# Moving the later modulation products beside the long convolutions and the scan

## The chip, the cores and the metric

The kernel runs on one core of a Trainium2 chip. The metric is the device time of one execution in microseconds; a time of a kernel is the median of its runs. The profile is of one further execution.

## The reference

Two layers of a trunk work on 1152 tokens (1024 latent, 128 prompt) of width 1024, in fp32. Each layer first computes six modulation vectors per condition (there are two conditions, `c` for latent tokens and `c_ctx` for prompt tokens), and then uses them around the token mixing and around the MLP:

```python
mod = einsum('bd,de->be', silu(cond), w_ada) + b_ada          # 1024 -> 6*1024
sh1, sc1, gt1, sh2, sc2, gt2 = split(mod, 6)
h = rms_norm(x, g_pre_mix) * (1 + sc1) + sh1
o = mixer(h)        # latent attention, windowed attention, gated delta scan, long convolutions
x = x + gt1 * rms_norm(o, g_post_mix)
h = rms_norm(x, g_pre_mlp) * (1 + sc2) + sh2
m = square(relu(h @ mlp_w1)) @ mlp_w2
x = x + gt2 * rms_norm(m, g_post_mlp)
```

`w_ada` is 1024 x 6144 per layer, 24 MB in fp32, and serves two rows of input: there is much to load and little to compute.

## The kernel before

The program is traced from Python and laid out by a planner. Every instruction goes to a fixed engine; the planner orders each engine's instructions by the order in which the Python code emitted them and by when it believes their inputs and buffers to be ready, and adds the waits. SP issues all DMAs, in its own order. On the chip each engine then works through its fixed list.

**Modulation products.** `ada(l, g)` (line 386) computes group `g` of layer `l`: 2048 columns, that is two of the six vectors. Group 0 holds `sh1, sc1`, group 1 `gt1, sh2`, group 2 `sc2, gt2`. It takes eight steps, one per 128 rows of weights. A step loads four tiles `wada` of 128x512 (256 KB each) and multiplies each by the condition, which stands as a 128x32 weight tile; the four results go to four strips of 32 partitions of one PSUM tile from tag P, which stays taken until the group ends. A ninth step copies the result to a row (`adarow`), transposes it in four pieces (`adat`) and adds the bias. The tiles `wada` come from tag T, which has four buffers, or from the tag given.

**Order of emission.** In each layer `run_timed` (line 2149) emits three generators side by side. Each has a clock of its own; the one with the lowest clock goes next, and each `yield` moves its clock on by the number yielded, or by a default.
- `rest()` is the main line: projections (15 units for each tile), then `hyena` (line 1682, two long convolutions through DFT matmuls, 10 units a step, eleven steps), then `attention` (line 1003, 2 units a step). Attention's main part begins only when `"other"` is done.
- `other()` is the gated delta rule: filters, `gdn_prep` and `gdn_scan` (line 1292, 16 steps in sequence), 6 units a step, emitted with a priority raised by 300.
- `adas()` (line 2055) waits 580 units (`SIDE`) and then emits groups 1 and 2 of this layer at 12 units a step, which falls beside attention.

The first group of layer 0 is computed at the start of the kernel. The first group of layer 1 is emitted beside the MLP of layer 0 (lines 2128 and 2129), with `wada` in the six buffers of tag H. The MLP itself runs in 16 blocks of two 128-row tiles of hidden units.

**Names in the rows.** `ada`, `wada`, `wo` (weights of the output projection, staged in tag T by `load_rows`, line 236), `op` (the output projection's PSUM), `S` and `ST` (scores of latent attention, for the maximum and for the weights), `O` (its output), `u` and `St` (vector and state of the scan), `sc` (the scan's loaded operands), `hid` and `mo` (MLP). Tags P, T and H have 4, 4 and 6 buffers.

Of the kernel before, what the change touches and what calls it, by code (L numbers as in the profile page):

```python
# [19 lines left out]
DEPTH = 2  # L20
# [7 lines left out]
GD = 6  # L28
PL = 4
AT = 2  # L30
SIDE = 580
NCH = ((0, 384), (384, 384), (768, 384))


# [130 lines left out]
class Trunk:  # L165
# [1830 lines left out]
    def layer(self, l):  # L1996
# [31 lines left out]
        def filters(tag, psum, h=None):  # L2028
            if h is None:
                h = self.W(name="sines", tag=tag)  # L2030
                nc.sync.dma_start(out=h[64 * l:64 * l + 64], in_=self.fscr[64 * l:64 * l + 64])
            for _ in self.hy_filters(l, h, self.dft_mats("fwd", tag), tag, psum):
                yield 8
# [15 lines left out]
        g, be = self.gdn_shared(l, gab, self.gdn_tag)  # L2049
# [2 lines left out]
                self.late_consts()  # L2052
        self.done = set()

        def adas():
            yield SIDE
            for a in (1, 2):
                yield from self.ada(l, a)

        def until(x):  # L2060
            while x not in self.done:
                yield 1

        def rest():
            yield from self.proj_gdn(l, hi, lo, (2, 4, 0), gcw, head)
            self.done.add("gdn0")
            yield from self.proj_rest(l, hi, lo, gab, gcw)
            self.small, self.other = R[0][-1], R[1][-1]
            first = self.mla_prep(l, 0)
            yield from self.hyena(l, self.sink(l), lambda: next(first))  # L2070
            yield from self.attention(l, first)

        def other():
            yield from filters(self.gdn_tag, "Q") if l else early
            yield from until("gdn0")
            self.pair = {}
            yield from self.gdn_prep(l, 0, g, be, self.gdn_tag)
            yield from until("gdn")
            yield from self.gdn_prep(l, 1, g, be, self.gdn_tag)
            yield from until("z")  # L2080
            yield from self.gdn_scan(l, self.gdn_tag)
            self.done.add("other")

        def ahead(g):
            while True:
                with self.tc.high_priority(300):
                    t = next(g, "end")
                if t == "end":
                    return
                yield t  # L2090
        run_timed((rest(), 1.5), (ahead(other()), GD), (adas(), 12))
        self.small, self.other = R[0][-1], R[1][-1]
        op = self.out_proj(l, R[1])
        if "oT" in self.dbg and l == self.dbg.get("l", 1):
# [18 lines left out]
        for ts in range(7):  # L2113
            g = op([ts])
# [4 lines left out]
        g = op([7, 8])  # L2119
        out = next(g)  # L2120
        self.run((g, 1), (group(0, xs[0:3]), 1), (group(1, xs[3:6]), 1))
        g = self.mlp(l, hi, lo)
# [2 lines left out]
        next(g)  # L2125
        self.run((group(2, xs[6:]), 1))
        acc = next(g)
        nxt = self.ada(l + 1, 0, "H") if l + 1 < DEPTH else iter(())
        self.run((g, 1), (nxt, 0.7))
        gate2 = {}  # L2130

        def tail(t):
# [16 lines left out]
def run_timed(*gens):  # L2149

    gens = [[0.0, i, g, n] for i, (g, n) in enumerate(gens)]
    while gens:
        e = min(gens)
        try:
            t = next(e[2])
            e[0] += e[3] if t is None else t
        except StopIteration:
            gens.remove(e)
# [33 lines left out]
```

## Time and profile before

| | us |
|---|---|
| median of 3 runs (3913.01 to 3923.71) | 3920.94 |
| the profiled execution | 3901.65 |
| its span, first to last instruction | 3899.9 |
| TensorE busy in the span | 3570.1 |
| VectorE busy | 2260.8 |
| ScalarE busy | 1359.3 |
| GpSimd busy | 848.4 |

All rows below are of the profiled execution, and their times count from the first instruction. A mean granted clock of 1.00 is 2.4 GHz; a lower mean says that the engine stood at the 1.2 GHz level for a part of the stretch. TensorE's matmuls overlap in their pipeline and their ends are modelled, so the time from one start to the next is the better measure of what a matmul takes.

### The profile page before, as it was taken

To read this page: it belongs to the slowest core of one execution; us is meant where nothing else is said; L and a number is where in the kernel's file an instruction comes from. 1 tells how busy PE (TensorE), PEld (TensorE's weight loads), DVE (VectorE), ACT (ScalarE), POOL (GpSimd) and SP (SyncE) were. 2 spreads that over 40 slices of the span, in tenths; PEclk is the share of its full clock that TensorE was granted. 3 is DMA by queue.
4 is the path that set the end of the run, shared out by engine and by line. 5 is a ranking of instruction groups with operands and counts; after the bars stand their busy time and mean duration, and the time that the engine had idled before them with its cause. 6 is when DMAs were issued, how large, how long until landed. Compare 5 with 4: busy or idle time off the path is not lost. (4 is left out here: it accounts for less than half of the span.)

```text
span 3899.9 us, 57406 instructions
## 1 busy us (share of the span) xinstructions
PE 3570.1 (92%) x21674; PEld 2999.4 (77%) x21674; DVE 2260.8 (58%) x4583; ACT 1359.3 (35%) x2932; POOL 848.4 (22%) x806
## 2 busy tenths in 40 slices
PE   7989887799999999999979897768998999999997
PEld 4889765566689888888868886556565899999996
DVE  5766478776454444444566674878664544444446
ACT  5434433445442222112354343324454422222122
POOL 1152421454230000000131633225542200000003
PEclk9999886799999999999989998768999999999999
DMA  5355462452621111111234365633525211111113
GB/s 202 113 130 155 147 231 88 123 138 73 207 77 64 55 62 44 59 53 55 80 112 140 105 164 150 212 109 93 154 72 194 71 55 44 44 44 41 41 41 116
DMA packets 366399, 405.30 MB, mean 104 GB/s; under 512 B 116007, under 2 KB 237349, under 8 KB 366122
## 3 DMA queue, kind: packets, MB, share of 16 engines
q1 hardware_dynamic: 366122, 401.64, 33.6%
q8 instruction: 170, 2.79, 0.3%
q14 instruction: 107, 0.88, 0.1%
HBM read 298.34 MB, written 103.19 MB: 103 GB/s over the span
## 5 line engine op out<-in xcount | busy, mean ns | idle before, releaser
L214 PE MATMUL hid<-hT,w1h 128*128 128x384 f32 x3072 | 787.2, 335 | 0.1
L1821 DVE TENSOR_TENSOR acc<-acc,mo 128x512 f32<-128x512 f32 x540 | 370.0, 687 | 435.3 <-PE mo L214 435.2
L214 PE MATMUL pj<-hT,wah 128*128 128x384 f32 x2112 | 575.1, 349 | 10.2 <-ACT hc L517 7.8
L214 PEld LDWEIGHTS hid<-hT,w1h 128*128 128x128 f32 x3072 | 557.5, 188 | 21.6 <-issue 6.7
L214 PE MATMUL hid<-hT,w1l 128*128 128x384 f32 x1536 | 514.4, 335 | 0.0
L214 PE MATMUL mo<-w2h,uh 128*128 128x512 f32 x1152 | 450.8, 391 | 1.4 <-DVE acc L1821 1.4
L214 PE MATMUL mo<-w2l,uh 128*128 128x512 f32 x1152 | 451.1, 392 | 0.0
L214 PE MATMUL mo<-w2h,ul 128*128 128x512 f32 x1152 | 450.8, 392 | 0.0
L214 PEld LDWEIGHTS pj<-hT,wah 128*128 128x128 f32 x2112 | 392.6, 194 | 24.0 <-ACT hc L517 8.8
L270 POOL TENSOR_TENSOR postr<-postr,mhalf 128x1 f32<-128x1 f32 x36 | 22.4, 625 | 1642.7 <-DVE postr L269 903.3
L660 POOL TENSOR_TENSOR e<-e,e 128x512 f32<-128x512 f32 (+1 forms) x216 | 296.9, 1376 | 331.3 <-ACT e L649 215.3
L214 PE MATMUL pj<-hT,wal 128*128 128x384 f32 x1056 | 365.3, 346 | 0.7 <-DVE wal L233 0.7
L214 PEld LDWEIGHTS hid<-hT,w1l 128*128 128x128 f32 x1536 | 288.2, 188 | 2.5
L233 DVE TENSOR_TENSOR el<-e,eh 128x512 fp32r<-128x512 f32 (+1 forms) x252 | 247.3, 1002 | 57.8 <-ACT eh L651 54.1
L243 ACT CAST w2h<-w 128x512 fp32r<-128x512 f32 x128 | 71.2, 618 | 524.9 <-PE mo L214 520.8
L214 PEld LDWEIGHTS mo<-w2h,ul 128*128 128x128 f32 x1152 | 216.2, 188 | 47.3
L1803 ACT ACTIVATE relu<-hid 128x384 f32<-128x384 f32 x192 | 93.9, 489 | 443.4 <-PE hid L214 443.4
L214 PEld LDWEIGHTS mo<-w2h,uh 128*128 128x128 f32 x1152 | 216.4, 188 | 41.4 <-DVE acc L1821 1.8
L214 PEld LDWEIGHTS mo<-w2l,uh 128*128 128x128 f32 x1152 | 216.2, 188 | 38.8
L214 PEld LDWEIGHTS pj<-hT,wal 128*128 128x128 f32 x1056 | 205.0, 194 | 4.6 <-issue 2.0
L1804 DVE SCALAR_TENSOR_TENSOR relu<-hid,relu 128x384 f32<-128x384 f32 x192 | 106.2, 554 | 164.6 <-ACT relu L1803 164.4
L233 DVE TENSOR_TENSOR wal<-wa,wah 128x512 fp32r<-128x512 f32 x88 | 67.8, 772 | 166.3 <-ACT wah L254 132.3
(488 smaller groups left out, 6357.0 us busy)
## 6 DMA issues: line engine op xcount, KB each, us to landing
w<-in_w SPq DMA_DIRECT2D x256, 256.0 KB
wada<-in_w_ada SPq DMA_DIRECT2D x192, 256.0 KB
wa<-in_wa SPq DMA_DIRECT2D x88, 256.0 KB
x<-in_x SPq DMA_DIRECT2D x18, 512.0 KB
Q<-rscr SPq DMA_DIRECT2D x32, 288.0 KB
o<-oscr SPq DMA_DIRECT2D x18, 512.0 KB
xres<-x SPq DMA_DIRECT2D x36, 256.0 KB
x<-xres SPq DMA_DIRECT2D x36, 256.0 KB
```

The source lines that it names most:

```text
L214: self.last = self.nc.tensor.matmul(out, l, r, start=start, stop=stop, skip_group_check=True)
L233: self.nc.vector.tensor_tensor(out=lo, in0=x, in1=hi.bitcast(F32), op=ALU.subtract)
L243: self.nc.scalar.copy(out=hi[:, q], in_=st)
L270: self.nc.gpsimd.tensor_tensor(out=out, in0=out, in1=self.bcs(self.mhalf[:out.shape[0]], out.shape), op=ALU.pow)
L660: self.nc.gpsimd.tensor_tensor(out=acc, in0=acc, in1=e, op=ALU.add)
L1803: nc.scalar.activation(out=r[:, :n], in_=ps[:, :n], func=AF.Relu)
L1804: nc.vector.scalar_tensor_tensor(out=r[:, :n], in0=ps[:, :n], scalar=0.0, in1=r[:, :n], op0=ALU.max, op1=ALU.mult)
L1821: nc.vector.tensor_tensor(out=acc[t][:, ns], in0=acc[t][:, ns], in1=ps, op=ALU.add)
```

## The change

Groups 1 and 2 of a layer no longer wait 580 units; they begin when the projections of the layer have been emitted (`"proj"`), and each step moves their clock on by 5 instead of 12. In layer 0, group 0 of layer 1 follows them there, in tag T, and is gone from beside the MLP.

```diff
-SIDE = 580
...
-        def adas():
-            yield SIDE
-            for a in (1, 2):
-                yield from self.ada(l, a)
-
         def until(x):
             while x not in self.done:
                 yield 1

+        def adas():
+            yield from until("proj")
+            for a in ((l, 1), (l, 2)) + (((l + 1, 0),) if l + 1 < DEPTH else ()):
+                for _ in self.ada(*a):
+                    yield 5
+
         def rest():
             yield from self.proj_gdn(l, hi, lo, (2, 4, 0), gcw, head)
             self.done.add("gdn0")
             yield from self.proj_rest(l, hi, lo, gab, gcw)
+            self.done.add("proj")
...
-        run_timed((rest(), 1.5), (ahead(other()), GD), (adas(), 12))
+        run_timed((rest(), 1.5), (ahead(other()), GD), (adas(), 1))
...
-        nxt = self.ada(l + 1, 0, "H") if l + 1 < DEPTH else iter(())
-        self.run((g, 1), (nxt, 0.7))
+        self.run((g, 1))
```

## Rows read from the trace of the kernel before

**Rows 1.** The page: 40 slices of 97.5 us, TensorE busy and clock, tenths.

```profile
PE   7989887799999999999979897768998999999997
...
PEclk9999886799999999999989998768999999999999
```

**Rows 2.** Stretches: length; busy PE, PEld, DVE, ACT, POOL; clock; DMA share; GB/s.

```profile
530.00:704.00 174.00, 112.33 (x1102) 87.56 (x1102) 135.27 (x417) 52.47 (x179) 36.43 (x38) 0.69 0.48 150
760.00:816.00 56.00, 54.10 (x266) 42.45 (x265) 49.68 (x70) 33.75 (x63) 35.31 (x24) 0.94 0.36 83
816.00:847.00 31.00, 31.00 (x110) 13.62 (x109) 21.54 (x35) 10.94 (x21) 15.23 (x11) 1.00 0.51 155
869.00:896.00 27.00, 27.00 (x82) 10.71 (x81) 13.72 (x25) 11.52 (x20) 12.74 (x10) 1.00 0.36 107
954.00:1012.00 58.00, 58.00 (x252) 28.71 (x251) 29.31 (x42) 27.80 (x54) 24.50 (x21) 1.00 0.52 158
...
2460.00:2640.00 180.00, 116.00 (x1132) 89.72 (x1132) 135.33 (x420) 53.24 (x183) 37.33 (x38) 0.69 0.50 153
2753.00:2788.00 35.00, 35.00 (x121) 14.68 (x119) 24.39 (x41) 13.48 (x25) 15.61 (x11) 1.00 0.53 158
2806.00:2829.00 23.00, 23.00 (x68) 9.19 (x67) 12.67 (x20) 10.62 (x19) 11.91 (x9) 1.00 0.33 100
2890.00:2950.00 60.00, 58.81 (x255) 29.21 (x253) 29.90 (x45) 29.45 (x58) 24.86 (x21) 1.00 0.53 163
```

**Rows 3.** Tile ada: passes, ns min/median/max, first and last start; four stretches.

```profile
L214 PE MATMUL ada<-wada,cst x64: 592/617/1062, 12.7 to 38.5; 128*32 128x512 f32 x64
...
L214 PE MATMUL ada<-wada,cst x128: 592/605/617, 816.2 to 1011.6; 128*32 128x512 f32 x128
...
L214 PE MATMUL ada<-wada,cst x128: 592/605/617, 2753.5 to 2948.0; 128*32 128x512 f32 x128
...
L214 PE MATMUL ada<-wada,cst x64: 592/605/617, 1282.9 to 1772.7; 128*32 128x512 f32 x64
```

**Rows 4.** Timeline of TensorE in attention: start, us, instruction; two pieces, their followers.

```profile
816.25 1.07 PE L214 MATMUL ada<-wada,cst 128*32 128x512 f32 x8
817.25 0.73 PE L214 MATMUL ST<-Q,K 97*128 97x512 f32 x2
...
822.24 1.04 PE L214 MATMUL ada<-wada,cst 128*32 128x512 f32 x2
823.22 0.45 PE L214 MATMUL S<-K,Q 96*128 96x384 f32 x1
```

**Rows 5.** Tiles hid and mo: first and last matmul of each layer's MLP.

```profile
L214 PE MATMUL hid<-hT,w1h x1536: 333/334/445, 1126.7 to 1912.5; 128*128 128x384 f32 x192
L214 PE MATMUL mo<-w2h,ul x576: 387/393/473, 1139.8 to 1938.2; 128*128 128x512 f32 x192
...
L214 PE MATMUL hid<-hT,w1h x1536: 331/334/443, 3079.1 to 3853.5; 128*128 128x384 f32 x192
L214 PE MATMUL mo<-w2h,ul x576: 387/389/475, 3092.1 to 3879.8; 128*128 128x512 f32 x192
```

**Rows 6.** End of attention: SP's timeline, stretches as in 2, and TensorE's longest wait.

```profile
2940.08 1.74 SPq L393 DMA_DIRECT2D wada<-in_w_ada  x2
2942.89 1.97 SPq L242 DMA_DIRECT2D wo<-in_w_out  x2
...
1012.00:1050.00 38.00, 35.03 (x154) 27.33 (x154) 17.43 (x32) 16.61 (x31) 3.65 (x4) 0.96 0.85 288
2948.00:3000.00 52.00, 40.62 (x159) 28.45 (x158) 23.06 (x42) 21.87 (x43) 8.20 (x8) 0.93 0.71 246
...
PE op L214 <- ACT woh L243: 5.7, 7, 2.0
```

**Rows 7.** Waits from 530 to 704 us: total us, times, longest; SP, then TensorE.

```profile
SPq L1374 <- DVE sc L1371: 22.6, 5, 10.8
...
PE u L214 <- DVE u L1352: 10.1, 6, 2.9
```

## Prediction

> **What bounds the kernel now.** I read the page's slices first: TensorE stands at 9 all through the later attention and the MLP, and falls to 6 and 7 in slices 7 and 8 and again in 26 and 27, where the long convolutions and the scan of each layer run; the granted clock falls there too [rows 1]. Then the table by stretches. From 530 to 704 us and from 2460 to 2640 us, where the convolutions stand beside the scan, TensorE is busy 112.3 of 174 us and 116.0 of 180 us at a mean granted clock of 0.69, so part of the time at the 1.2 GHz level, while VectorE is busy 135 us in each (75 to 78%) [rows 2]. In the stretches of attention that hold the modulation products TensorE is busy all or nearly all of the time at full clock and VectorE only half to 70% [rows 2]. In the MLP TensorE is the bound outright [rows 1]. So the change takes TensorE work out of stretches that TensorE bounds and puts it where TensorE stands idle for 61.7 and 64.0 us.
>
> **What a product costs today.** One group of products is 32 matmuls of 512 columns, each shown as two passes. A layer has 128 passes in its attention, and 64 more lie in the first layer's MLP [rows 3]. Four matmuls write four different strips of 32 PSUM partitions; issued together they take 1.00 us up to the start of the next instruction (816.25 to 817.25), and a single one takes 0.98 us (822.24 to 823.22) [rows 4]. What counts is therefore the number of pieces. The timeline shows the 128 passes of a layer's attention in 52 pieces, 27 of the first group and 25 of the second: in each group one piece of eight passes, two or four of four, the rest of two. The reason is the buffers: weights come through the four slots of tag T, a slot is loaded again only when its matmul is done, and each matmul runs as soon as its load lands. In the MLP all eight pieces hold eight passes.
>
> **Part by part.** 1. *Out of attention.* 104 pieces of 0.98 us are 102 us of TensorE time, the most that can come back. Not all will, since VectorE comes next: where no product runs, at 760 to 816 us, it is busy 49.68 of 56 us, 89%, and I take that as its practical limit [rows 2]. For each stretch I take the larger of two floors: its TensorE time without the pieces, and its VectorE time over 0.887. 816 to 847 us has 15 pieces: 31 − 14.7 = 16.3 against 21.54/0.887 = 24.3, so 6.7 us saved. 869 to 896 has 12: 15.2 against 15.5, so 11.5 saved. 954 to 1012 has 25: 33.5 against 33.0, so 24.5 saved. In layer 1 the same working gives 7.5 (17 pieces), 8.7 (10) and 24.5 (25). Sum 83 us.
> 2. *Out of the MLP.* The MLP of layer 0 runs from 1126.7 to 1938.2 us, that of layer 1, which has no products in it, from 3079.1 to 3879.8: 811.5 − 800.7 = 10.8 us [rows 5]. I take 10, with 8 (eight pieces) to 11 as bounds.
> 3. *Ahead of the output projection.* Its weights are staged in the same four T slots. In layer 1 the first of these loads goes out at 2942.89, right behind the last pair of modulation loads at 2940.08, and TensorE then waits for the cast of these weights; it is idle 11.4 us from 2948 to 3000 and 3.0 us from 1012 to 1050 [rows 6]. With the slots free earlier, these loads can go out as soon as their own buffers are free. I take half, 7 us, with 0 and 14 as bounds.
> 4. *Into convolutions and scan.* Layer 0 gets three groups there (its own two and the next layer's first), layer 1 gets two. The products begin when the projections have been emitted and step by 5 on the emission clock against the convolutions' 10, so 27 steps take 135 units against the 110 of the convolutions: the last fifth of layer 0's products falls beside the start of attention. The slots are the same four, so I expect the same single pieces: 3 × 26 × 0.98 = 76 us in layer 0 and 2 × 26 × 0.98 = 51 us in layer 1. Idle are 61.7 and 64.0 us: by the sum 14 us spill over in layer 0 and nothing in layer 1. To this I add collisions: TensorE takes its instructions in order, and a matmul of the scan that comes ready during a piece waits on average half of it. I estimate that half of the 130 pieces meet one, 130 × 0.5 × 0.49 = 32 us. Together about 45 us. Bounds: below, −10 us, since VectorE alone needs 135.3/0.887 = 152 us of the 174 and a fuller TensorE may hold the 2.4 GHz level longer; above, 127 us if no piece is hidden, and more while the clock is low (the longest pass at the start of the kernel took 1062 ns against a median of 605 later [rows 3]). I take 45 because the idle time is measured and large; it needs the pieces to fall into it.
> 5. *Small things.* The copy, four transposes and two additions that end a group go with it and cost nothing next to this. The modulation loads pass SP's queue of that stretch: 96 issues in layer 0 and 64 in layer 1, 24 and 16 MB, against a DMA share of 0.48 and 0.50 there [rows 2]; the bandwidth is there on the mean, and its cost is in the 45. One PSUM bank of the four of tag P is held for a whole group, now away from the convolutions instead of away from attention. The convolutions evacuate with VectorE, which is the slower side anyway: nothing.
> Sum: 83 + 10 + 7 − 45 = 55 us. The profiled execution took 3901.65 us, 0.5% under the median of 3920.94; I carry the difference over in us: 3901.65 becomes about 3847, the median about **3866**.
>
> **Two rules of the Trainium skill.** The pieces stand in the rows as said: four together 1.00 us, one alone 0.98 [rows 4]. The Trainium skill, "TensorE: Matmul & The Clock Gate", Part 3, says that matmuls on different column strips run at once, so that a pack takes one matmul's time plus a few ns for each further one; the rows agree. By that rule 24 full packs in layer 0 and 16 in layer 1 would cost about 40 us of TensorE time in place of 127, and all would be hidden: that is the first rival.
> Of SP the rows show that it stands waiting in this stretch already, 22.6 us in five waits for one of the scan's VectorE results alone [rows 7]. The Trainium skill, "DMA: Bandwidth & Descriptors", section "Anatomy of one DMA", says that DMA engines never wait on semaphores and that the issuing sequencer waits before dispatch; by that a modulation load that waits for its slot would hold the loads behind it. That speaks against the change and is the last rival.
>
> **The rivals.**
> *All hidden.* The products pack, or their pieces all fall into idle time, and the higher clock pays for the collisions: 100 + 5 to 15 us come back, about 3815. For it: the idle time of TensorE, and a clock of 0.69 that can rise. Against it: the same ring of four slots made 26 pieces of a group in both layers' attention.
> *A wash.* The pieces lie on the scan's chain rather than beside it. In this stretch TensorE waits six times, 10.1 us in all, for VectorE's u of the scan [rows 7], so the two hand over in turn, and each piece in between costs its full 0.98 us, with the clock low at times: 95 to 110 us of cost against 100 of gain, 3911 to 3931.
> *Not as said.* The emission order is not the order on the engines: a planner places every instruction when it thinks it ready. If it puts most pieces into the first 110 us of attention, where VectorE is at 89%, only the MLP, the projection's start and some of the later stretches gain: 15 to 35 us, 3886 to 3906.
> *SP becomes the bound, slower.* A load of modulation weights waits at the head of SP's queue for a slot that a TensorE matmul frees; behind it stand the filter spectra that a convolution multiplies by, the scan's own loads and its stores. The scan or the convolution stands still until the slot comes. There are 24 + 16 steps of four loads, and the ring turns once in about 5.6 us (two pairs of loads stand 2.81 us apart [rows 6]). Against 100 us of gain it decides from 2.5 us of standstill in each step; at 4 us it gives 40 × 4 = 160 − 100 = 60 us more, 3980. Against it: the spectra come through a pool of six buffers, and in attention, with the same ring beside it, TensorE was busy all of the time.
>
> **How the numbers follow.** About 0.3%, 12 us, is what a measurement of this kernel can tell from no change. Chances: the forecast, 3841 to 3890, 0.50; all hidden, 3805 to 3841, 0.27; not as said 0.06; a wash 0.08; SP as the bound 0.09. Faster by over 0.3% is the first three, 0.83; within 0.3% the wash, 0.08; slower 0.09. The range runs from 3810 to 3912: it leaves out the slow rival (0.09), most of the wash (0.06) and the lowest part of the all-hidden case (0.05).
>
> **What would show it.** Step 1: no modulation piece in attention outside its first tens of us, attention 35 to 50 us shorter in each layer, VectorE near 89% throughout. Step 2: the MLPs of both layers equally long. Step 3: the output projection's weights loaded before attention ends, and less idle TensorE at its start. Step 4: the stretch of convolutions and scan 25 to 35 us longer in layer 0 and 10 to 20 in layer 1, TensorE nearly full there, its granted clock above 0.69, and its waits for the scan's VectorE results gone or replaced by pieces. I am wrong if these stretches grow by as much as attention shrinks, or if SP's waits there are for the modulation's slots.

## The result and the profile after

The changed kernel takes 3877.68 us (median of 4 runs, 3860.68 to 3886.40) against 3920.90 (4 runs): ratio 0.9885, 95% interval 0.9856 to 0.9914. The forecast of 3866 is 12 us too low and the range holds. The profiled execution took 3886.40 us, the longest of its four, so its difference to the profiled execution of before (3901.65, 19 us under its median) is only 15 us, where the medians differ by 43. A second profile (below, `again`) repeats its rows to within 4 us in each of the stages that are compared here.

The stages, cut at the first or last matmul of the tiles `pj` (projections), `ST`, `op`, `hid` and `mo`, in us of the two profiled executions:

| stage | layer 0 before | after | layer 1 before | after | change, both | forecast |
|---|---|---|---|---|---|---|
| projections and before | 530.2 | 535.4 | 521.1 | 528.0 | +12.1 | 0 |
| convolutions and scan | 174.1 | 192.3 | 182.4 | 190.4 | +26.2 | +45 |
| attention | 309.1 | 281.4 | 308.1 | 306.3 | −29.5 | −83 |
| output projection to first `hid` | 113.3 | 110.8 | 129.3 | 117.4 | −14.4 | −7 |
| MLP | 811.4 | 800.1 | 800.7 | 803.6 | −8.4 | −10 |

The page's slices, which answer to [rows 1]: TensorE has filled up in slices 7 and 8, and its clock falls in other slices than before, 9 and 10 and 28 to 30, which are attention.

```profile
PE   7989888899999999999979888878999999999997
PEclk9989888887999999999989898887859999999999
```

The stretch table of the changed kernel (length; busy PE, PEld, DVE, ACT, POOL with counts; granted clock; DMA share; GB/s): convolutions and scan of layer 0, attention of layer 0, then the same of layer 1.

```profile
535.43:727.78 192.35, 151.06 (x1274) 85.70 (x1273) 139.79 (x428) 54.07 (x181) 35.99 (x38) 0.82 0.77 245
727.78:1009.22 281.44, 270.19 (x1143) 191.90 (x1142) 215.78 (x349) 154.74 (x297) 154.98 (x107) 0.87 0.34 89
...
2448.08:2638.51 190.43, 145.53 (x1271) 85.82 (x1270) 138.33 (x429) 55.03 (x188) 37.43 (x38) 0.83 0.73 234
2638.51:2944.81 306.30, 286.14 (x1108) 210.82 (x1108) 220.99 (x355) 154.24 (x297) 151.22 (x108) 0.75 0.26 66
```

The two stretches of attention before, cut in the same way:

```profile
704.35:1013.42 309.07, 300.80 (x1253) 191.09 (x1253) 212.51 (x350) 153.56 (x292) 148.97 (x108) 0.91 0.39 109
2641.64:2949.75 308.11, 299.86 (x1252) 189.05 (x1252) 214.80 (x351) 153.58 (x292) 147.97 (x108) 0.92 0.39 107
```

In layer 1 all 52 pieces have left attention, 51 us of TensorE work by the prediction's price, and it is 1.8 us shorter. The clock says where they went. A stretch times its mean granted clock is the time at full speed that it was granted: 308.11 × 0.92 = 283 us before, 306.30 × 0.75 = 230 after. The engine was given 54 us less for 51 us less work, so it took as long. In layer 0 the same product falls by 36 us for 34 pieces, but from 0.91 to 0.87 only, and there 28 us came back.

How it falls is seen in stretches of 8 us in the changed kernel's layer 1 (same columns):

```profile
2748.00:2756.00 8.00, 7.77 (x36) 6.25 (x34) 8.00 (x12) 7.73 (x15) 5.88 (x5) 1.00 0.01 2
2756.00:2764.00 8.00, 4.88 (x14) 2.49 (x14) 8.00 (x10) 1.74 (x4) 6.43 (x4) 0.82 0.00 1
2764.00:2772.00 8.00, 7.79 (x22) 5.49 (x22) 4.40 (x11) 3.03 (x7) 1.68 (x2) 0.50 0.14 41
...
2812.00:2820.00 8.00, 6.13 (x18) 3.35 (x18) 6.89 (x12) 1.70 (x3) 2.15 (x2) 0.74 0.00 0
2820.00:2828.00 8.00, 7.63 (x23) 5.42 (x21) 5.16 (x15) 3.51 (x8) 2.08 (x2) 0.50 0.01 2
...
2876.00:2884.00 8.00, 8.00 (x27) 5.98 (x27) 4.77 (x11) 3.01 (x5) 3.73 (x3) 0.50 0.00 0
```

VectorE is full from 2748 to 2764, and TensorE, which waits five times for VectorE's `el` (0.46 to 0.78 us each by the timeline), is busy 4.88 of 8 us; the clock drops to the 1.2 GHz level. Then the work turns to TensorE (VectorE 4.4 of 8), and it is done at half speed until 2788. The same happens at 2812 (VectorE busy 6.89 us, TensorE 6.13, its longest wait for `el` 1.13), and this time all eight stretches from 2820 to 2884 are at 0.50 with TensorE busy 7.6 to 8.0 of 8 us. Before, pieces stood just there, and TensorE was full at 1.00:

```profile
2756.00:2764.00 8.00, 8.00 (x31) 4.25 (x30) 7.76 (x11) 5.67 (x11) 5.89 (x5) 1.00 0.54 173
2764.00:2772.00 8.00, 8.00 (x27) 3.06 (x23) 5.91 (x7) 1.28 (x3) 3.09 (x2) 1.00 0.51 161
...
2812.00:2820.00 8.00, 8.00 (x28) 3.72 (x27) 3.19 (x5) 2.41 (x4) 2.14 (x3) 1.00 0.31 98
```

The matmuls are slower there too, by 1.4 times, where the mean clocks of this stretch, 0.87 before and 0.50 after, would make 1.7; their ends are modelled, so the clock's own rows count for more. By shape, from 2820 to 2880 us (count; busy us, mean ns; idle before), first after, then before:

```profile
L213 PE MATMUL sS<-sK,sQ 64*128 64x384 f32 x11 | 6.8, 650 | 0.0
L213 PE MATMUL sO<-eh,sVA 128*128 128x512 f32 x7 | 5.0, 720 | 0.0
```

```profile
L214 PE MATMUL sS<-sK,sQ 64*128 64x384 f32 x15 | 6.8, 465 | 0.5 <-DVE smx L909 0.5
L214 PE MATMUL sO<-eh,sVA 128*128 128x512 f32 x9 | 4.7, 523 | 0.0
```

The products and their loads in the changed kernel: tile `ada` in either layer, answering to [rows 3]; TensorE's and SP's longest waits for them from 535 to 765 us (total us, times, longest), answering to [rows 7]; and the loads of the output projection's weights in layer 1, answering to [rows 6].

```profile
L213 PE MATMUL ada<-wada,cst x192: 592/617/1063, 535.7 to 764.0; 128*32 128x512 f32 x192
...
L213 PE MATMUL ada<-wada,cst x128: 592/617/1063, 2448.3 to 2607.2; 128*32 128x512 f32 x128
...
PE ada L213 <- DMA wada<-in_w_ada: 13.7, 11, 4.2
...
SPq L392 <- PE ada L213: 49.5, 36, 5.9
...
L241 SPq DMA_DIRECT2D wo<-in_w_out x16: 327/354/545, 2606.3 to 2914.5; - x16
```

By the timeline, counting passes that follow each other as one piece, 152 passes in 32 pieces lie in layer 0's convolutions and scan and 40 passes in 18 pieces at the start of its attention; in layer 1 all 128 passes lie in 33 pieces, where attention had 52.

### The profile page after: what moved, and what is told of

It is laid out like the page before. It is cut to its first block, busy times and chain, and to the rows that moved or that the text cites. A ratio compares the mean times of both kernels' runs of the same rounds, so it can differ in the third digit from the quotient of the medians.

```text
span 3884.3 us, 57351 instructions
## 1 busy us (share of the span) xinstructions
PE 3592.5 (92%) x21674; PEld 3028.9 (78%) x21674; DVE 2267.7 (58%) x4583; ACT 1356.6 (35%) x2932; POOL 855.1 (22%) x806
## 5 line engine op out<-in xcount | busy, mean ns | idle before, releaser
L213 PEld LDWEIGHTS hid<-hT,w1h 128*128 128x128 f32 x3072 | 557.4, 188 | 13.7 <-ACT h L478 1.1
L659 POOL TENSOR_TENSOR e<-e,e 128x512 f32<-128x512 f32 (+1 forms) x216 | 307.1, 1423 | 318.2 <-ACT e L648 174.8
```

The source lines that it names most:

```text
L213: self.last = self.nc.tensor.matmul(out, l, r, start=start, stop=stop, skip_group_check=True)
L659: self.nc.gpsimd.tensor_tensor(out=acc, in0=acc, in1=e, op=ALU.add)
```

## The experiments

The theory from the two traces: the pieces had kept TensorE's clock up in attention, so what their removal gives back depends on the clock and not only on the work. Rivals: something else holds attention up (the casts of the output projection's weights, transfers), or the products cost more beside the convolutions than their stage shows.

**Pricing what is left of the products.** `cut` computes one of the eight steps of every group but the kernel's first, and so leaves out seven eighths of the other products with their loads.

```diff
-        for kt in range(8):
+        for kt in range(8 if l == g == 0 else 1):
...
```

> The changed kernel with the products cut to one of their eight steps in every group but the very first, so seven eighths of the modulation products are left out and their loads with them: the pieces are neither in attention nor beside the convolutions. Changed kernel for comparison: convolutions and scan (last projection matmul to first ST) 193 us in layer 0 and 191 in layer 1; attention (first ST to first op) 281 and 306 us; kernel before 174, 182 and 309, 308. Both theories: the stretches of convolutions and scan fall back to about 174 and 182 us, since the pieces cost 19 and 8 us there. Clock theory (the pieces held TensorE's clock up in attention): attention's granted clock stays as low as in the changed kernel, stretches at 0.50, and layer 1's attention stays at 295 to 310 us; total 3840 to 3860. Rival (attention without pieces is what my floors said, and something else that the move brought, the loads or the order, made it long): attention falls to 265 to 275 us in both layers; total 3790 to 3815.

Measured 3849.15 us (3840.17 to 3859.33), ratio 0.9828 (0.9803 to 0.9854): by the ratios 22 us and by the medians 29 us less than the changed kernel, which is what these products still cost. By stages they cost 9.1 us in the convolutions of layer 0 and 15.5 in those of layer 1 (183.3 and 175.0 us; 174 and 182 were expected, so only the sum came back). The stages and the total agree, so the rival of a higher price than the stage shows falls. Attention gives nothing: 283.9 us in layer 0, without the 18 pieces, and 306.2 in layer 1, at 0.78 and 0.76. That layer 1 is 22 us longer than layer 0 at nearly the same clock is hardly the clock's doing; VectorE is busy 26 us longer in it.

```profile
717.71:1001.62 283.91, 270.45 (x1088) 200.71 (x1088) 207.93 (x338) 154.00 (x296) 150.89 (x107) 0.78 0.24 59
2612.50:2918.71 306.21, 282.45 (x1118) 207.65 (x1119) 234.16 (x385) 157.23 (x301) 154.53 (x109) 0.76 0.27 71
```

**Giving TensorE something to do.** A filler is one fp32 matmul of a score tile into an unused PSUM bank that nobody reads. `warm512` puts one of 512 columns after every third full score tile, 38 a layer; `warm128` one of 128 columns after each, 114 a layer.

```diff
+        self.fed += 1
+        if self.fed % 3 == 0 and n == 512:
+            self.mm(self.feed[0:32, :512], self.cst[:, 0], e[:, :512])
```

> The changed kernel with idle work added: after every third score tile of attention one fp32 matmul of 512 columns into a PSUM strip that nobody reads, about 40 a layer of 0.98 us, with no load. It is about what the pieces were, without their loads. Clock theory: the granted clock of attention rises from stretches at 0.50 to 0.95 or more, and attention takes no longer than in the changed kernel, 290 to 308 us in layer 1, although TensorE has 40 us more to do. Rival (VectorE and the chain of exponentials bound attention, and the low clock costs nothing): no gain from the clock, and each layer's attention longer by what of the 40 us does not hide, 10 to 40 us; total 3900 or more.

> As the kernel with 512 columns, but after every full score tile one matmul of 128 columns: about 120 a layer of some 0.25 us, 30 us of TensorE work a layer, spread evenly. Clock theory: attention at a clock above 0.9 and 10 to 20 us a layer shorter than in the changed kernel, total 3840 to 3860. Rival: attention 5 to 30 us a layer longer, total 3890 or more.

`warm512`: 3877.75 us (3867.74 to 3878.74), ratio 0.9895 (0.9876 to 0.9914), the time of the changed kernel, with 76 more passes in each layer. Layer 1's attention is 15.7 us shorter than without them, at 0.90 (0.95 or more was expected), layer 0's 7.7 us longer, at 0.97. `warm128`: 3915.66 us (3904.97 to 3942.60), ratio 0.9995 (0.9973 to 1.0017), a miss: attention is 27 and 18 us longer than in the changed kernel, as its rival had it. The tile `feed`, first of `warm512`, then of `warm128` (ns min/median/max):

```profile
L213 PE MATMUL feed<-e,cst x152: 592/617/1062, 730.9 to 2924.1; 128*32 128x512 f32 x152
```

```profile
L213 PE MATMUL feed<-e,cst x456: 272/297/423, 731.0 to 2987.3; 128*32 128x128 f32 x152
```

These durations overlap the next matmul's. From its start to that of the next instruction, a large filler takes 0.98 us and a small one 0.34 at the full clock (medians over both layers); one of each, `warm512` first:

```profile
2712.79 1.04 PE L213 MATMUL feed<-e,cst 128*32 128x512 f32 x2
2713.76 0.44 PE L213 MATMUL S<-K,Q 96*128 96x384 f32 x1
...
2740.82 0.41 PE L213 MATMUL feed<-e,cst 128*32 128x128 f32 x2
2741.16 0.97 PE L213 MATMUL ST<-Q,K 97*128 97x512 f32 x3
```

So the small fillers add 114 × 0.34 = 39 us a layer against 38 × 0.98 = 37, nearly the same work, and the miss is not one of work alone. In layer 1, 324.12 × 0.83 = 269 us at full speed were granted against 290.61 × 0.90 = 262, so 33 us more time went into 7 us more work. The same work in small portions kept the clock up less well; why is open. Layer 1, `warm512` and then `warm128`:

```profile
2638.31:2928.92 290.61, 283.00 (x1184) 185.40 (x1185) 224.07 (x353) 158.90 (x298) 155.96 (x108) 0.90 0.27 69
```

```profile
2664.45:2988.57 324.12, 320.49 (x1336) 210.91 (x1336) 222.44 (x351) 160.34 (x299) 151.74 (x107) 0.83 0.23 58
```

**The same filler where the clock is up already.** `bwarm512` adds the lines of `warm512` to the kernel before.

> The kernel before, with the same unread filler: one fp32 matmul of 512 columns into 32 unused PSUM partitions after every third full score tile of attention, about 40 us of TensorE work in each layer at the full clock. Nothing is left out. Theory (the products kept TensorE's clock up in attention, and the filler is free only where the clock would otherwise fall): in the kernel before the granted clock of attention is 0.82 to 1.00 already and TensorE is the bound there, so the filler has nothing to buy and costs most of itself: 20 to 40 us a layer, 3950 to 4000. Rival (the filler is free because attention has idle cover for it on TensorE, whatever the clock): 3910 to 3930, attention 305 to 315 us in both layers.

Measured 3958.01 us (3956.45 to 3959.58), ratio 1.0097 (1.0066 to 1.0128), as the theory said. Attention grows to 339.6 and 339.9 us, by 31 us a layer; 339.95 × 0.95 = 323 us at full speed against 283 are 40 us more, near the filler's 38 × 0.98 = 37. So the same work costs 31 us a layer where TensorE is full at 0.92, and nothing in the sum where its clock was 0.75 to 0.87. That is the strongest evidence for the theory.

```profile
2673.67:3013.62 339.95, 335.38 (x1329) 190.04 (x1329) 217.05 (x348) 158.39 (x292) 147.10 (x108) 0.95 0.36 98
```

**Half of the products left in attention.** `split` computes groups (l, 1) and (l + 1, 0) beside the convolutions and group 2 beside attention.

```diff
-            for a in ((l, 1), (l, 2)) + (((l + 1, 0),) if l + 1 < DEPTH else ()):
+            for a in ((l, 1),) + (((l + 1, 0),) if l + 1 < DEPTH else ()):
                 for _ in self.ada(*a):
                     yield 5
+            yield 100
+            for _ in self.ada(l, 2):
+                yield 12
```

> The change, with the second modulation group of each layer left beside attention, in paced steps, and only the first group and the next layer's first beside the convolutions. Nothing is left out. Clock theory: the 32 steps in attention are work that has to be done somewhere and feed the clock as they did before: attention 280 to 295 us in both layers (306 in layer 1 of the changed kernel), convolutions and scan 5 to 10 us shorter a layer than in the changed kernel, the total 3850 to 3872. Rival (a product in attention costs its TensorE time as the prediction had it, clock or not): attention 15 to 25 us longer a layer than in the changed kernel, the convolutions 5 to 10 us shorter, the total 3885 to 3905.

Measured 3903.24 us (3897.22 to 3913.06), ratio 0.9964 (0.9941 to 0.9986): the total of the rival, but not by its reason. Convolutions and scan are 9.5 and 7.7 us shorter than after, as both had it. Layer 1's attention is 304.7 us, 1.6 us shorter than after, where the rival had 15 to 25 more. Layer 0's is 318.8 us, longer even than before with twice the products. Its last product starts at 898.3:

```profile
896.00:904.00 8.00, 8.00 (x30) 4.62 (x30) 4.90 (x8) 4.33 (x9) 3.95 (x3) 1.00 0.46 151
904.00:912.00 8.00, 6.63 (x25) 3.92 (x23) 8.00 (x17) 6.04 (x11) 4.16 (x4) 0.89 0.21 66
912.00:920.00 8.00, 7.74 (x21) 5.02 (x21) 5.85 (x16) 0.75 (x3) 0.66 (x1) 0.50 0.01 2
...
968.00:976.00 8.00, 8.00 (x33) 7.16 (x32) 3.82 (x8) 4.26 (x8) 2.76 (x2) 0.50 0.00 0
```

While the pieces run (805 to 898 us) the clock is 0.95 and TensorE full, so they cost their time; then VectorE is full for one stretch, the clock falls, and 64 us at 0.50 follow with TensorE full. My theory had 280 to 295 us for both layers. It missed that half of the dose can lose both ways, as in layer 0: the pieces do not help what comes after them.

**The third group back beside the MLP.** `keep10` undoes that part of the change.

```diff
-            for a in ((l, 1), (l, 2)) + (((l + 1, 0),) if l + 1 < DEPTH else ()):
+            for a in ((l, 1), (l, 2)):
...
-        self.run((g, 1))
+        nxt = self.ada(l + 1, 0, "H") if l + 1 < DEPTH else iter(())
+        self.run((g, 1), (nxt, 0.7))
```

> The change, with the third group (the next layer's first) left beside the MLP of layer 0 as in the kernel before. Nothing is left out. By the prediction's step 2 the MLP of layer 0 is 10 to 12 us longer again, 811 us. What it gives back tells what the third group costs where the change puts it: by the prediction's price (26 pieces of 0.98 us, part of them in idle time) convolutions, scan and attention of layer 0 are 10 to 20 us shorter than in the changed kernel, the total 3868 to 3880. Rival (the third group is hidden in the convolutions, or its 18 pieces at the start of attention hold the clock there): these stretches stay within 4 us, the total 3884 to 3892.

Measured 3907.04 us (3871.04 to 3913.98), ratio 0.9954 (0.9928 to 0.9979), which neither had. The MLP of layer 0 is 811.3 us again, as step 2 says. Convolutions, scan and attention of layer 0 take 485.6 us against 473.8 with the group there: 7 less in the convolutions, 19 more in attention, whose clock is 0.77 and 0.50 from 900 to 940 us. `cut`, with no piece there either, had 283.9 us at 0.78, so not all of the 19 is clock: each kernel is planned anew, and such a difference between two plans stays unexplained.

**The output projection's weights.** `hold` issues their loads only behind attention's last store.

```diff
-                nc.sync.dma_start(out=dst, in_=src)
+                self.out_last = nc.sync.dma_start(out=dst, in_=src)
...
-        Wo = [self.load_rows(...) for k in range(8)]
+        with self.tc.issue_after(self.out_last.ins):
+            Wo = [self.load_rows(...) for k in range(8)]
```

> The change, with the loads of the output projection's weights held back until the last store of attention has been issued. Nothing is left out. In the changed kernel these loads and their casts are spread over attention. By the prediction's step 3 the early loads are what shortens the start of the projection (14.3 us in both layers together, measured): held back, that start is as late as before or later, op to hid 125 to 140 us in each layer, attention unchanged, the total 3890 to 3910. Rival (the casts that the early loads bring into attention cost VectorE and ScalarE there as much as the early start saves, and are why attention of layer 1 has not become shorter): attention of layer 1 is 10 to 20 us shorter, the total 3865 to 3880.

Measured 3920.30 us (3902.49 to 3930.03), ratio 1.0000 (0.9977 to 1.0022). The total is above its range, and the stage from `op` to `hid` takes 118.1 us, under the 125 to 140 expected, and 130.1: 20 us more than after in the two layers together. TensorE waits 12.3 us for casts of these weights in layer 1 again. Attention is not shorter (297.9 and 305.2 us), so the early casts are not what holds it up: the rival falls. Layer 0's attention was to be unchanged; why it is 16.5 us longer here is open.

```profile
PE op L213 <- ACT woh L242: 12.3, 5, 6.1
```

**More slots.** `ring` loads groups 1 and 2 into twelve slots (tags T and L) in place of four.

```diff
-                for _ in self.ada(*a):
+                for _ in self.ada(*a, "TLLL" if a[1] else "T"):
```

> The changed kernel with the loads of groups 1 and 2 taken from the eight idle buffers of tag L beside the four of tag T. Ring theory (single pieces come from four slots that are refilled one at a time): the 128 passes of a layer's two groups fall in packs of eight, 16 to 20 pieces in place of about 36, and the stretches of convolutions and scan shrink from 193 and 191 us towards 180 and 184; total 10 to 25 us under the changed kernel. Rival (VectorE and the DMAs bound these stretches, the number of pieces does not matter): fewer pieces, but the stretches within 5 us of those of the changed kernel.

Measured 3866.09 us (3848.83 to 3873.06), ratio 0.9883 (0.9865 to 0.9902), within the interval of the changed kernel. The products come in 43 pieces in layer 0, not 50, and in 22 in layer 1, not 33. SP's waits for the slots from 535 to 765 us fall from 49.5 to 17.7 us. Yet the convolutions take 200.4 us in layer 0, 8 more than after, and 186.4 in layer 1, 4 less: the waits were not the bound. The profiled execution, one of its short ones, has layer 1's attention at 281.4 us and a clock of 0.83, with no piece and no filler in it:

```profile
2631.28:2912.69 281.41, 262.58 (x1108) 194.70 (x1109) 219.25 (x351) 154.86 (x298) 156.42 (x108) 0.83 0.28 71
```

So attention without pieces need not take the 306 us of the changed kernel. Where the clock falls, and for how long, also hangs on the plan, and no run here separates the two.

**Another execution, and fillers in chosen places.** `again` is the changed kernel once more. `head` puts 14 fillers at the first 14 score tiles of layer 1's attention, `mid` 21 in each layer at every third tile from the 36th to the 96th.

```diff
+        self.fed += n == 512
+        if n == 512 and self.fed in self.fills:
+            self.mm(self.feed[0:32, :512], self.cst[:, 0], e[:, :512])
...
+        self.fills = range(1, 15 if l else 1)   # head
+        self.fills = range(36, 97, 3)           # mid
```

> The changed kernel once more, unaltered, beside the next two on one chip, so that another of its executions is profiled. Theory (what differs between its executions is how far TensorE's granted clock falls in attention): the median 3870 to 3885; if the profiled execution is a shorter one than the 3886.4 us of the first, its attention is shorter with a higher granted clock, and the other stretches are within 3 us. Rival (the executions differ by transfers or waits outside attention): attention within 5 us of the first profile, and the difference in the convolutions or in the projections.

> The change, plus 14 unread filler matmuls (fp32, 512 columns, 32 PSUM partitions, some 17 us of TensorE time) at the first 14 full score tiles of layer 1's attention, where layer 0 has the last 18 pieces of its third group. Nothing is left out. Theory (dense TensorE work at the start of attention is why layer 0's attention stayed short and kept its clock, 281 us against 306 in layer 1): layer 1's attention falls to 283 to 295 us with a granted clock near 1.00 in its first 40 us and above 0.6 later, the total 3860 to 3870. Rival (the start does not matter for what follows): the filler adds 5 to 17 us to layer 1's attention, 305 to 320 us, the total 3880 to 3895.

> The change, plus 21 fillers of the same kind in each layer, at every third full score tile from the 36th to the 96th of 114, where the granted clock falls to 0.50 in the changed kernel (some 25 us of TensorE time a layer). Nothing is left out. Theory (the filler only pays where the clock would fall): the clock of the later half of attention is 0.80 or more, attention 272 to 290 us in both layers, the total 3855 to 3870. Rival (once the clock is low, a third of the fillers no longer lifts it, and they only add work): attention 285 to 320 us, the total 3885 to 3905.

`again`: 3892.28 us (3875.55 to 3898.88), ratio 0.9898 (0.9865 to 0.9930); the median is above the 3870 to 3885 of its expectation. The profiled execution (3889.83) was no shorter, so it does not tell the two apart; attention is 282.8 and 305.9 us, within 1.4 us of the first profile. Over the ten executions of the changed kernel a longer time goes with a lower mean granted clock, from 3860.68 us at 0.933 to 3898.88 at 0.921; that is a correlation and names no cause.

`head`: 3879.52 us (3870.33 to 3887.22), ratio 0.9870 (0.9838 to 0.9901). Attention of layer 1 is 302.1 us, outside the theory's numbers and the rival's. The start runs at 0.90 and then 1.00, but from 2820 to 2860 the clock is 0.61 all the same, against 0.50 after: a dense start carries little over. The 14 fillers show no cost.

```profile
2650.00:2700.00 50.00, 48.22 (x166) 28.54 (x164) 35.72 (x50) 20.99 (x38) 21.81 (x15) 0.90 0.14 35
2700.00:2740.00 40.00, 37.58 (x187) 28.19 (x186) 36.41 (x53) 24.02 (x46) 24.57 (x16) 1.00 0.17 44
...
2820.00:2860.00 40.00, 39.07 (x137) 28.84 (x137) 23.22 (x52) 16.38 (x35) 12.73 (x10) 0.61 0.10 26
```

`mid`: 3871.27 us (3858.14 to 3889.04), ratio 0.9858 (0.9822 to 0.9894), 1 us over its range and 21 us under `again` on the same chip, though the two intervals overlap. Layer 1's attention is 280.4 us at 0.88, 26 us shorter than without the 21 fillers; layer 0's is 293.3 at 0.91, 12 us longer and 3 over its range. The profiled execution is the shortest of its six.

```profile
2638.67:2919.06 280.39, 269.18 (x1150) 187.10 (x1151) 220.29 (x351) 157.04 (x299) 155.16 (x108) 0.88 0.27 69
```

**Both together.** `ringmid` has the twelve slots, and the 21 fillers in layer 1 alone.

```diff
+        self.fills = range(36, 97, 3) if l else ()
...
+                for _ in self.ada(*a, "TLLL" if a[1] else "T"):
```

> The change with the ring of 12 slots for the products' weights and, in layer 1 alone, the 21 fillers of the run before (every third full score tile from the 36th to the 96th). Nothing is left out. Theory (both are small gains in different stretches, the ring in the convolutions, the filler by the clock of layer 1's attention): layer 0's attention 275 to 285 us, layer 1's 275 to 285 with a clock of 0.85 or more, the total 3845 to 3865. Rival (they do not add: the clock in the ring's attention of layer 1 is high enough in most executions, so the filler only adds work): layer 1's attention 285 to 300 us, the total 3868 to 3885.

Measured 3856.62 us (3844.09 to 3866.10), ratio 0.9836 (0.9808 to 0.9864), as the theory said to 0.1 us: attention 274.9 and 282.0 us, both at 0.89. But layer 1's attention took 281.4 us in `ring` without the fillers, at 0.83, so that they gained something here is not shown. It has the lowest median of the kernels that compute everything, about 0.5% under the changed one; its interval overlaps that of `mid`, touches that of the changed kernel's first series and lies just clear of the second.

## Why the prediction was right, and where its terms were wrong

The time lies in the range and the direction is right, but two terms of the sum were far off and partly cancelled. That the median came within 12 us is partly luck: in the two profiled executions the stages give back 14 us of the 55, and the other 29 of the median's 43 stand in no stage that a profile shows.

**Step 1, attention, −83 forecast, −29.5 measured: the step that failed.** Of its predicted 43 and 41 us, layer 0 gave 28 and layer 1 gave 2. The failing part is the floors: I took TensorE's time without the pieces at the clock of the stretch, 1.00 in the chosen rows [rows 2]. Those rows are at 1.00 with the pieces in them; the row without pieces, 760 to 816 us, was at 0.94. The stretches between the pieces, which I did not show, were lower still, with VectorE at 72 to 74%:

```profile
896.00:954.00 58.00, 56.92 (x274) 42.57 (x274) 41.83 (x97) 31.68 (x67) 22.64 (x19) 0.85 0.11 29
2829.00:2890.00 61.00, 59.88 (x283) 43.64 (x282) 45.39 (x99) 32.59 (x69) 23.92 (x20) 0.86 0.10 27
```

Without pieces the phases that VectorE bounds leave TensorE idle, its clock falls, and the phases that TensorE bounds then take longer. `cut` (no piece, no further gain), `bwarm512` and `warm512` (the same filler, 31 us a layer or nothing) show that what such work costs or gives back hangs on the clock, and `mid` shows it in one layer at the place itself. Not all fits: `warm128` did not keep the clock up with as much work, and `ring` has a shorter layer 1 with none. I had no rival for it. "VectorE near 89% throughout" was wrong too: it is busy 215.78 of 281.44 us, 77%, and 220.99 of 306.30, 72%.

The Trainium skill, "TensorE: Matmul & The Clock Gate", section "HAM oscillation — how this bites in real kernels", says that TensorE is throttled again when it waits between groups of matmuls, so that the next group starts at the low clock. The rows at 2756 and 2812 agree: the clock falls behind waits, here of 0.5 to 1.1 us each. The Trainium skill, in Part 1 of the same page, says that sustained activity releases the throttle; the rows from 2820 to 2884 us do not show that, with TensorE busy 7.6 to 8.0 of each 8 us at 0.50, and the measurement decides. A full row has modelled ends, though, and need not mean that the engine worked without a break.

**Step 2, the MLP, −10: right.** Layer 0 gave 11.3 us, and `keep10` puts 11.2 back. That the other MLP is 2.9 us longer lies outside the change: it has no product in either kernel.

**Step 3, the output projection, −7 forecast, −14.4 measured:** the upper bound, not half of it. The loads go out from 2606 us on, all within attention or ahead of it, and `hold` takes the gain away and more.

**Step 4, convolutions and scan, +45 forecast, +26 measured.** The mechanism was right: the spill is 18 pieces at the start of attention, as reckoned; the clock rises from 0.69 to 0.82 and 0.83; TensorE is fuller, busy 151 of 192 us, if not nearly full. The size was too large because the products come in 50 and 33 pieces and not in 78 and 52: by the prediction's own term 83 × 0.5 × 0.49 = 20 us of collisions and no overflow. That the faster clock pays for some collisions as well is not shown. `cut` agrees: without nearly all products the two stretches are 25 us shorter. (The 6 and 7 that the prediction reads for TensorE in slices 7 and 8 are the clock's; TensorE stands at 7 in both, and nothing hangs on it.)

**The rivals.** "All hidden" fails on both sides: 26 us of cost remain, and 100 us never came back. "SP as the bound" does not hold, though the sign that I named for it came: SP's longest waits in this stretch are for the slots, 49.5 us in all, and TensorE waits 13.7 us for the weights. `ring` removes most of the first without gain. "Not as said" came true for the 18 pieces alone. "A wash" had engines that take turns as its reason; that is where the loss came from, but in attention.

**What stays open.** The projections are 5 and 7 us longer; over the other kernels the second lies between 520 and 528 us, so this is within what plans and executions differ by. What raises the clock again with TensorE no busier (at 2788 us, for instance) no row shows. Nor does any run show where the executions of before spend the 19 us between the profiled one and their median.

## What to carry to other kernels

Before moving work off TensorE, look at what the clock does in the rows without that work, not only in those with it: a stretch at 1.00 may owe it to the very instructions to be moved. Where two engines take turns as the bound, filler work on TensorE can be free. Half of the products left in place can be worse than all or none, as in layer 0's attention of `split`, though not in the total. Price such a step with one run that adds idle work to the kernel before and one that leaves the moved work out.

## What the runs showed of the hardware

TensorE stood at the 1.2 GHz level for 64 us in a row while its rows were full (2820 to 2884 us after, 912 to 976 us in `split`), each time right after one stretch of 8 us in which VectorE was busy 6.9 to 8.0 us and TensorE 6.1 to 6.6 us. And an fp32 matmul into 32 partitions (two passes) took 0.34 us at 128 columns against 0.98 at 512, from its start to the next one's, so four small ones cost 1.4 times one large one.
